# First FFN half of a two-layer backbone: weight sums formed by accumulating transfers in device memory, with modulation sums and mixer folds in their place on VectorE

## The chip, the cores and the metric

The kernel runs on one core of a Trainium2 chip. The metric is the device time of one execution in microseconds; for each kernel the median of several executions counts. TensorE (PE) does the matrix products, VectorE (DVE) and ScalarE (ACT) the elementwise work, SyncE (SP) issues transfers. GpSimd (POOL) has hardly any work in this kernel. "PEld" in the profile is TensorE's loading of weights, which overlaps its products.

## The reference

One step of a backbone of two layers over 128 context and 512 latent tokens, D = 1024. Every layer is a half-step SwiGLU FFN, a token mixer and a second half-step FFN, each between two RMS norms with shift, scale and gate from a modulation of the conditioning vectors. The mixer of the first layer is a two-dimensional Fourier transform between two projections, that of the second is attention.

```python
def _modulation(cond, w_mod, b_mod):
    m = jax.nn.silu(cond) @ w_mod + b_mod
    return m.reshape(cond.shape[0], N_MOD, D_MODEL)

def _swiglu(h, w1, w2):
    gate, up = jnp.split(h @ w1, 2, axis=-1)
    return (jax.nn.silu(gate) * up) @ w2

def _half_ffn(x, m, k, g_pre, g_post, w1, w2):
    h = _modulated_prenorm(x, g_pre, m, k)
    return x + 0.5 * m[:, 3 * k + 2, None] * _rmsnorm(_swiglu(h, w1, w2), g_post)

def _fourier_mix(h, w_in, w_out):
    b, s, _ = h.shape
    u = (h @ w_in).reshape(b, s, N_FOURIER_GROUPS, FOURIER_GROUP_DIM)
    f = jnp.fft.fft2(u.astype(jnp.float32), axes=(1, 3), norm="ortho").real
    return f.astype(h.dtype).reshape(b, s, D_MODEL) @ w_out

for i in range(DEPTH):
    m_ctx = _modulation(c_ctx[None, :], w_mod[i], b_mod[i])
    m_lat = _modulation(c, w_mod[i], b_mod[i])
...
    if i % N_MIXERS == 0:
        yp = _fourier_mix(hp, four_w_in[j], four_w_out[j])
        ys = _fourier_mix(hs, four_w_in[j], four_w_out[j])
...
```

Context and latent tokens are separate sequences in the Fourier mixer and share its weights. The FFN's inner width is 2816, that is 22 f tiles of 128.

## The kernel before, in words

**Arithmetic.** Every float32 operand is split into a high and a low part (`split`, lines 260 and 261: ACT copies the high part, DVE subtracts it), and a product is three matrix products (`mm3`, lines 274 to 276). So each weight tile passes three steps before PE can use it: SP loads a raw tile of 128 x 1024 (512 KB, line 203, "raw<-in_w" and the like in the profile), ACT writes "hi", DVE writes "lo". The raw tiles are a ring of four (NRAW), the split pairs a ring of six (NWU). `unit(i)` returns a pair and sends the ones up to three ahead through `send`, in the order of `list_units`. The results of products that are operands of later ones are split in the same way; "ring", "left", "right", "square", "total" and "rms" are names of such buffers, "main", "score", "turn" and "sum" are accumulator banks.

**First FFN half (n = 0).** Its plan is written out in `plan_ffn`. The first f tiles are done by the direct method; from f = 3 on, `w1_fast` forms the two halves of a hidden tile with seven products in place of eight, on sums of weights and sums of activations. Of the raw gate and up tiles of an f tile, four sums of 128 x 512 are needed, three for the unit "sums" (lines 228 to 230) and one for the unit "all" (line 243), all DVE's. After f = 4, 8, 12 and 16 a slice of four f tiles of w2 is run over the five token tiles, and at the end the last six.

**Background.** The modulation (the sums over `w_mod`) is cut in 128 jobs. A job loads one raw tile and runs two reductions of 1024 columns on DVE (line 478, "junk<-raw,wide"). They are taken from a list by `behind`: 36 of them between the w2 products of the first FFN half, four at its end; three in `pair_in(1)` and five in the loop over `channels`; the rest in the other sub-layers (BEHIND).

**Mixer of the first layer (n = 1).** `pair_in(0)` multiplies latent tiles 0 and 1 with the eight tiles of `four_in`, then come the context tile's odd and even products and `pair_in(1)`. Then, for each of four parts m, `positions` transforms along the tokens and `channels` along the channels, with splits of each result between the products. Then `four_out` follows: `pair_out(1)`, the context tile and `pair_out(0)`, each with its norm and its residual (`boundary`). The weights of `four_in` and `four_out` are folded when they are loaded, with two DVE operations for each (lines 237 and 238). A boundary on POOL's part takes the root of the norm (line 610), and line 633 writes the normalised tile for the next sub-layer.

**What sets the order.** The order in which instructions stand on an engine follows from the order in which the code issues them and from `high_priority` and `behind_of` around some of them; a scheduler sorts the rest by when they are expected to be ready. Each engine runs its queue in order, so that an operation which waits holds up all that stand behind it.

Of the kernel before, what the change touches and what calls it, by code (L numbers as in the profile page):

```python
# [43 lines left out]
BEHIND = (36, 0, 36, 36, 0, 8)  # L44
TURNS = (
# [107 lines left out]
class Kernel:  # L153
# [59 lines left out]
    def send(self, kind, src):  # L213
# [18 lines left out]
        elif kind.startswith("fold"):  # L232
            raw = self.raw_tile(src)
            a, b = raw[:, one], raw[:, two]
            if "rows" not in kind:
                a, b = a.rearrange("p (m c) -> p m c", m=4)[:, :, 2:], raw[:, 520:].rearrange("p (m c) -> p m c", m=4)
            nc.vector.tensor_tensor(b, a, b, op=ALU.subtract)
            nc.vector.scalar_tensor_tensor(out=a, in0=a, scalar=2.0, in1=b, op0=ALU.mult, op1=ALU.subtract)
        elif kind == "up":
            raw = self.fast["up"]  # L240
        else:
            raw, at = self.fast["gate"], two
            nc.vector.scalar_tensor_tensor(out=raw[:, two], in0=self.fast["sums"][:, two], scalar=-1.0,
                                           in1=raw[:, two], op0=ALU.mult, op1=ALU.subtract)
        n = at.stop - at.start
        if kind in ("block", "foldblock", "foldrowsblock"):
# [4 lines left out]
        return hi, lo  # L251

# [360 lines left out]
    def chain(self, n, i, pss, acc=()):  # L613
# [66 lines left out]
        with high():  # L680
# [33 lines left out]
            if n == 0:  # L714
                j, n_pieces = tiles[0], 2 * len(tiles)
                y = self.staged[:, 2 * j : 2 * j + n_pieces][:, :: -1 if j == CTX_TILE else 1]
# [4 lines left out]
                if i in (1, 2):  # L721
                    v, t, col = (2, SPECIAL, TOK + 1) if i == 1 else (5, 0, TOK)
                    for c in range(0, NCH, 2):
                        hi, lo = (h.block(part, c, 0)[:, :, col] for part in range(2))
                        self.split(hi, lo, self.staged[:, v, c : c + 2, t])
# [13 lines left out]
    def ffn(self, layer, which, base, boundary):  # L739
# [45 lines left out]
        def combine(step):  # L785
# [16 lines left out]
            if step < 2:  # L802
                t = combine.now[k] = [self.temp(("square", "total")[step]).rearrange(shape, **sizes) for _ in range(2)]
                steps = ((1, t[0], b12, b11), (2, t[1], b22, t[0]))
            else:
                t = combine.now[k]
                steps = ((3, t[0], b22, b12), (4, t[1], t[1], b21))
            for i, to, a, b in steps:
                if k == 0:
                    sums[i] = [quad(self.ring(F32R)) for _ in range(2)]  # L810
                nc.vector.tensor_tensor(to, a, b, op=ALU.subtract)
# [37 lines left out]
        def w1_fast(f, ahead):  # L849
# [28 lines left out]
            with high():  # L878
                tt(a, a, w, op=ALU.add)
# [10 lines left out]
            with high():  # L890
                nc.vector.scalar_tensor_tensor(out=q, in0=w, scalar=-1.0, in1=q, op0=ALU.mult, op1=ALU.subtract)
# [24 lines left out]
        def w2(s, tiles):  # L916
# [33 lines left out]
        for op, a, half in plan:  # L950
# [81 lines left out]
    def list_units(self):  # L1032
        io = self.io
        self.bases = []
        self.plans = {}
        for i in range(DEPTH):
            for sub in range(3):
                self.bases.append(len(self.units))
                if sub != 1:
# [3 lines left out]
                    for op, v, j in self.plans[n][1]:  # L1043
                        if op == "w2":
                            self.units.append(("plain", io["w2"][i, sub // 2, v + j]))
                        elif op in ("w1", "w1up"):
                            self.units.append(("block" if v == 3 else "plain", w1[v, int(op == "w1up")]))
                        elif op in ("sums", "again"):
                            self.units.append((op, (w1[v, 0], w1[v, 1])))
# [3 lines left out]
                if i == 0:  # L1053
                    self.units += [("foldblock" if k >= NWU else "fold", io["four_in"][k]) for k in range(NCH)]
                    self.units += [("plain", io["dft"][k]) for k in range(3)]
                    self.units += [("foldrowsblock" if u in (3, 4) else "foldrows", io["four_out"][u]) for u in range(NCH)]
# [24 lines left out]
    def fourier(self, base, boundary):  # L1081
# [44 lines left out]
        for k in range(NCH):  # L1126
            even_in(k, token(k, LAT + 64, TOK + 2), even)
# [45 lines left out]
        def positions(m):  # L1173
            ps = sums(m)
            p = [self.temp("left", F32R)[:, :322] for _ in range(2)]
            self.split(*p, ps)
            ps = diffs(m)
            q = [self.temp(kind, F32R)[:126, :384] for kind in ("square", "total")]
            self.split(*q, ps)
            return p, q  # L1180

        def channels(m, p, q):
# [6 lines left out]
            self.split(*even_at(m, 0, 322), ps)  # L1189
            ps = self.bank("score")[:, :384]  # L1190
            self.mm3(ps, mid_w[0][:126, P : 2 * P], mid_w[1][:126, P : 2 * P], *q, True, True)
            self.split(*odd_at(m, 0, 384), ps)
# [577 lines left out]
```

## Time and profile before

| | |
|---|---|
| median of three runs | 2219.53 us (2216.15 to 2219.59) |
| the profiled execution, its own time | 2218.44 us |
| its span, first to last instruction | 2216.7 us |
| mean granted TensorE clock | 0.988 |
| PE busy, DVE busy, ACT busy, POOL busy | 2173.2, 1743.1, 1179.2, 45.3 us |
| DMA traffic | 293.25 MB, mean 132 GB/s |
| first FFN half | until about 426 us |
| Fourier mixer | about 426 to 605 us |

The times come from one profiled execution. A row of the groups by line reads: line, engine, operation, output and inputs with shapes, count, then the time busy, the mean of one in ns, and the engine's idle time just before, with what ended it. A row of the table by stretches reads: the stretch and its length, the busy time (and count) on PE, PEld, DVE, ACT and POOL, the granted clock (1.00 is full), the busy share of the 16 DMA engines and their GB/s. A row of the timeline begins with the start and the duration; in square brackets stand the idle time before it and its releaser. Rows of DMA issues give the count, the size of one and the median time from issue to landing.

### The profile page before, as it was taken

The page shows a single profiled execution, that of the slowest core. Times are in us where ns is not written, and L with a number is a line of the kernel's source. Part 1 is how long each engine was busy: PE and PEld are TensorE (multiplying, and loading weights), DVE is VectorE, ACT ScalarE, POOL GpSimd, SP SyncE. Part 2 cuts the span into 40 slices and gives each one's busy share as a digit, 9 for nine tenths or more (in the row PEclk, how much of TensorE's full clock was granted, in tenths as well). Part 3 has the DMA queues.
Part 4 walks back from the last instruction along what each step waited for, and adds up shares of the span by engine and source line. Part 5 has one row for each costly group of instructions (what it writes and reads, how often), then busy time and mean ns, then how long its engine had stood idle before and what let it go on. Part 6 is the DMA issues. An engine that isn't in the chain of part 4 may idle for free.

```text
span 2216.7 us, 34573 instructions
## 1 busy us (share of the span) xinstructions
PE 2173.2 (98%) x13299; PEld 1997.3 (90%) x13299; DVE 1743.1 (79%) x3218; ACT 1179.2 (53%) x2221; POOL 45.3 (2%) x95
## 2 busy tenths in 40 slices
PE   7999999999899999999999999999999999999998
PEld 5999999977699999898998999989998899999997
DVE  5988898889798889878998898686556686766684
ACT  4544545464654545446544454466778654455452
POOL 0000000010100000001000000010000000000000
PEclk9999999998999999999999999999999999999999
DMA  8244344625324434452344444533333323322242
GB/s 315 86 143 162 134 152 139 216 86 178 116 96 138 159 132 147 148 196 99 109 147 146 141 143 146 179 99 101 111 101 110 119 81 105 115 95 77 95 129 100
DMA packets 85861, 293.25 MB, mean 132 GB/s; under 512 B 9696, under 2 KB 14656, under 8 KB 85568
## 3 DMA queue, kind: packets, MB, share of 16 engines
q1 hardware_dynamic: 85152, 290.39, 39.1%
q8 instruction: 104, 1.70, 0.3%
q10 hardware_dynamic: 544, 0.66, 0.1%
q14 instruction: 61, 0.50, 0.1%
HBM read 275.49 MB, written 11.58 MB: 130 GB/s over the span
## 4 chain that ended last, share of the span: by engine, by line
PE 89%; DVE 5%; ACT 3%; DMA 2%; issue 1%; POOL 0%; SPq 0%; DVEq 0%; POOLq 0%; ACTq 0%
PE main L275 12%; PE main L276 12%; PE main L274 12%; PE score L275 7%; PE score L276 7%; PE score L274 7%; PE turn L275 4%; PE turn L274 4%; PE sum L274 4%; PE sum L275 4%; PE turn L276 4%; PE sum L276 4%; DVE junk L478 1%; DMA raw<-in_w_mod_t 1%; PE sum L1569 1%
## 5 line engine op out<-in xcount | busy, mean ns | idle before, releaser
L260 ACT ACTIVATE hi<-raw 128x1024 fp32r<-128x1024 f32 (+1 forms) x388 | 371.1, 969 | 287.3 <-PE score L275 93.1
L261 DVE TENSOR_TENSOR lo<-raw,hi 128x1024 fp32r<-128x1024 f32 (+1 forms) x388 | 429.7, 1112 | 99.1 <-ACT hi L260 97.7
L274 PE MATMUL main<-hi,ring 128*128 128x512 f32 (+4 forms) x1089 | 412.3, 380 | 5.9 <-ACT hi L260 2.3
L275 PE MATMUL main<-lo,ring 128*128 128x512 f32 (+4 forms) x1089 | 410.8, 378 | 4.8 <-DVE lo L261 4.8
L276 PE MATMUL main<-hi,ring 128*128 128x512 f32 (+5 forms) x1089 | 410.3, 377 | 0.0
L478 DVE SCALAR_TENSOR_TENSOR junk<-raw,wide 128x1024 bf16<-128x1024 f32 x256 | 313.1, 1223 | 79.6 <-DMA raw<-in_w_mod_t 75.5
L276 PE MATMUL score<-ring,lo 128*128 128x320 f32 x916 | 283.4, 309 | 0.6 <-DVE lo L261 0.6
L275 PE MATMUL score<-ring,hi 128*128 128x320 f32 x916 | 283.7, 310 | 0.0
L274 PE MATMUL score<-ring,hi 128*128 128x320 f32 x916 | 283.3, 309 | 0.0
L274 PEld LDWEIGHTS main<-hi,ring 128*128 128x128 f32 (+2 forms) x1089 | 204.9, 189 | 47.9 <-ACT hi L260 3.6
L275 PEld LDWEIGHTS main<-lo,ring 128*128 128x128 f32 (+2 forms) x1089 | 205.9, 189 | 43.9 <-DVE lo L261 6.3
L276 PEld LDWEIGHTS main<-hi,ring 128*128 128x128 f32 (+2 forms) x1089 | 206.0, 189 | 40.5 <-issue 1.2
L274 PE MATMUL turn<-ring,hi 128*128 128x320 f32 x672 | 207.6, 309 | 3.0 <-ACT ring L260 2.9
L275 PE MATMUL turn<-ring,hi 128*128 128x320 f32 x672 | 208.3, 310 | 0.0
L274 PE MATMUL sum<-ring,hi 128*128 128x320 f32 x672 | 208.0, 310 | 0.1
L275 PE MATMUL sum<-ring,hi 128*128 128x320 f32 x672 | 207.8, 309 | 0.0
L276 PE MATMUL sum<-ring,lo 128*128 128x320 f32 x672 | 207.5, 309 | 0.0
L276 PE MATMUL turn<-ring,lo 128*128 128x320 f32 x672 | 207.0, 308 | 0.0
L942 ACT ACTIVATE y<-main 128x512 f32<-128x512 f32 x160 | 94.2, 591 | 208.2 <-PE main L276 207.0
L274 PEld LDWEIGHTS score<-ring,hi 128*128 128x128 f32 x916 | 172.4, 188 | 1.1
L276 PEld LDWEIGHTS score<-ring,lo 128*128 128x128 f32 x916 | 172.2, 188 | 1.0 <-DVE lo L261 1.0
L275 PEld LDWEIGHTS score<-ring,hi 128*128 128x128 f32 x916 | 172.3, 188 | 0.7
(318 smaller groups left out, 4138.8 us busy)
## 6 DMA issues: line engine op xcount, KB each, us to landing
raw<-in_w SPq DMA_DIRECT2D x272, 512.0 KB, 3.7
raw<-in_w_mod_t SPq DMA_DIRECT2D x128, 512.0 KB, 3.5
raw<-in_qkv SPq DMA_DIRECT2D x26, 512.0 KB, 3.5
spill<-ring SPq DMA_DIRECT2D x12, 640.0 KB, 3.3
ring<-spill SPq DMA_DIRECT2D x12, 640.0 KB, 7.4
raw<-in_bias SPq DMA_DIRECT2D x16, 448.0 KB, 3.7
first<-in_w_mod_k SPq DMA_DIRECT2D x8, 512.0 KB, 8.2
ring<-in_w_mod_k SPq DMA_DIRECT2D x8, 512.0 KB, 10.2
```

The lines of the kernel that those rows point to most:

```text
L260: a = self.nc.scalar.activation(hi, src, AF.Copy)
L261: self.last_split = a, self.nc.vector.tensor_tensor(lo, src, hi.bitcast(F32), op=ALU.subtract)
L274: mm(out, whi, xhi, start=start, stop=False)
L275: mm(out, whi, xlo, start=False, stop=False)
L276: self.latest = mm(out, wlo, xhi, start=False, stop=stop)
L478: last = self.nc.vector.scalar_tensor_tensor(out=self.junk, in0=raw, scalar=1.0, in1=self.wide[:, cond, :], op0=ALU.mult, op1=ALU.mult, ac ...
L942: nc.scalar.activation(place(i, a), ps[a], AF.Copy)
L1569: mm = nc.tensor.matmul(out, cache_v[:, ds] if k is None else v[c // 2][c % 2][:, slot, ds], probs, start=n == 0, stop=n == len(tiles) - 1)
```

## The change

For the first FFN half (`FAR = (0,)`), f tiles 5 to 21, the four weight sums are no longer DVE's. `far_sums` builds them in a tile of device memory for each f tile (four blocks of 128 x 512, the names far_78 to far_94 in the order's rows), in four stages issued from POOL: a put of four elements, taken from activations that must be there before (this holds the chain back until then), and four puts of 256 KB from the weights; two accumulating transfers from the weights; one from block to block; another one. `w1_fast(a)` issues stage 0 of f tile a + 5, stage 1 of a + 4, stage 2 of a + 3 and stage 3 of a + 2; the first tiles are begun after the third step of `combine`. SP then loads the unit "sums" from that memory as a plain tile, "up" in two pieces (one from it, one from the weights) and "all" as half a tile, 1.75 MB for an f tile in place of 1 MB. Some signs turn, so that a few operations are plain sums in place of scaled ones.

The folds of `four_in` become eight background jobs (`fold_in`): load, two DVE operations, and a write of 512 KB to device memory issued from POOL; the mixer then loads the folded tiles as they are. They are put into the list of background jobs at places 6, 12, 19, 25, 32, 38, 45 and 51. The first FFN half now takes 56 jobs (36 beside w2, one after each of 17 f tiles, three at the end): 48 modulation jobs and the eight folds. The mixer takes none. `four_out` is folded in the mixer as before.

Besides, in the mixer: the context tile's tokens are stored in reverse, with tables to match, so that one splitting of special columns goes; the odd product of `pair_in(0)` uses a bank of "score"; the splits in `positions` and `channels` are issued at high priority; `unit(at + 4)` is asked for ahead of `pair_out(1)`. PE's instructions stay the same in number and shape.

```diff
+FAR = (0,)
...
+    def fold_in(self, k):
+
+        raw = self.raw_tile(self.io["four_in"][k])
+        a, b = (t.rearrange("p (m c) -> p m c", m=4) for t in (raw[:, :512], raw[:, 520:]))
+        self.fold(a[:, :, 2:], b)
+        self.nc.gpsimd.dma_start(out=self.folded[k], in_=raw)
+
+    def far_sums(self, n, f, stage, passed):
+
+        one, two = slice(0, 512), slice(512, UNIT)
+        w1 = self.io["w1"][n // 3, n % 3 // 2, f] if (n, f) in self.far else None
+        put, add = self.nc.gpsimd.dma_start, partial(self.nc.gpsimd.dma_start, accum_op=ALU.add)
+        while w1 is not None and self.staged_sums.get((n, f), 0) <= stage:
+            t, at = self.far[n, f].rearrange("p (a k) -> p a k", a=4), self.staged_sums.get((n, f), 0)
+            if at == 0:
+                put(out=t[:1, :, :1], in_=passed[:1, 0, :4].bitcast(F32).unsqueeze(2))
+                for a, src in enumerate((w1[0][:, one], w1[0][:, one], w1[1][:, one], w1[0][:, two])):
+                    put(out=t[:, a], in_=src)
+            elif at == 1:
+                add(out=t[:, 2], in_=w1[1][:, two])
+                add(out=t[:, 0], in_=w1[1][:, one])
+            elif at == 2:
+                add(out=t[:, 1], in_=t[:, 2])
+            else:
+                add(out=t[:, 3], in_=t[:, 1])
+            self.staged_sums[n, f] = at + 1
...
-            nc.vector.scalar_tensor_tensor(out=raw[:, two], in0=self.fast["sums"][:, two], scalar=-1.0,
-                                           in1=raw[:, two], op0=ALU.mult, op1=ALU.subtract)
+            nc.vector.tensor_tensor(raw[:, two], self.fast["sums"][:, two], raw[:, two], op=ALU.add)
...
-                if n == 0 and s == len(SLICES) - 1 and tiles[0] == 0 and f < f0 + 4:
+                if n == 0 and s == len(SLICES) - 1 and tiles[0] == 0 and f < f0 + 3:
...
             elif op == "combine":
                 combine(a)
+                if a == 3:
+                    for stage in range(4):
+                        for f in range(7 if stage < 3 else 6):
+                            self.far_sums(n, f, stage, sums[4][0])
...
             elif op == "fast":
                 w1_fast(a, half)
+                for i in range(4):
+                    self.far_sums(n, a + 5 - i, i, g[a])
+                if n == 0 and a > 4:
+                    self.behind()
...
+                        elif n in FAR and op in ("sums", "up", "all") and (n, v, "again") not in self.plans:
+                            if op == "sums":
+                                self.far[n, v] = self.dram.tile([P, 2 * UNIT], F32, tag=f"far{n}_{v}", name=self.name("far"))
+                            t = self.far[n, v]
+                            self.units.append({"sums": ("plain", t[:, :UNIT]), "all": ("half", t[:, UNIT + 512 :]),
+                                               "up": ("pieces", (t[:, UNIT : UNIT + 512], w1[v, 1][:, 512:]))}[op])
...
-                    self.units += [("foldblock" if k >= NWU else "fold", io["four_in"][k]) for k in range(NCH)]
+                    self.folded = [self.dram.tile([P, UNIT], F32, tag=f"fold{k}", name=self.name("fold")) for k in range(NCH)]
+                    self.units += [("block" if k >= NWU else "plain", self.folded[k]) for k in range(NCH)]
...
-            es, o = [self.bank() for _ in range(2)], self.bank()
+            es, o = [self.bank() for _ in range(2)], self.bank("main" if p else "score")
             for k in range(NCH):
-                if p and k % 3 == 1:
-                    self.behind()
...
-            self.split(*p, ps)
+            with high():
+                self.split(*p, ps)
...
-            self.behind((2, 2, 1, 0)[m])
...
+        self.unit(at + 4)
         pair_out(1)
...
+        for k in range(NCH):
+            self.background.insert(6 + 13 * k // 2, partial(self.fold_in, k))
```

More of the change, by code (lines that the diff above doesn't have):

```diff
@@ L233, in send @@
             raw = self.raw_tile(src)
[L234 to L238, printed above, removed]
+            self.fold(raw[:, one], raw[:, two])
+        elif kind == "pieces":
+            raw = self.raw.tile([P, UNIT], F32, tag="raw", name=self.name("raw"))
+            for a, piece in zip((one, two), src):
+                nc.sync.dma_start(out=raw[:, a], in_=piece)
+        elif kind == "half":
+            raw, at = self.raw_tile(src, 512), one
         elif kind == "up":
@@ L720, in chain @@
                     self.ready = self.split(split(hi), split(lo), y[:, :, c : c + 2].rearrange("p v c t -> p c v t"))
-                if i in (1, 2):
-                    v, t, col = (2, SPECIAL, TOK + 1) if i == 1 else (5, 0, TOK)
+                if i == 1:
                     for c in range(0, NCH, 2):
-                        hi, lo = (h.block(part, c, 0)[:, :, col] for part in range(2))
-                        self.split(hi, lo, self.staged[:, v, c : c + 2, t])
+                        hi, lo = (h.block(part, c, 0)[:, :, TOK] for part in range(2))
+                        self.split(hi, lo, self.staged[:, 2, c : c + 2, SPECIAL])
                 tiles = ()
@@ L878, in w1_fast @@
             with high():
-                tt(a, a, w, op=ALU.add)
+                tt(a, a, w, op=ALU.subtract)
             if f in opened:
@@ L1034, in list_units @@
         self.bases = []
-        self.plans = {}
+        self.plans, self.far, self.staged_sums = {}, {}, {}
         for i in range(DEPTH):
@@ L1126, in fourier @@
         for k in range(NCH):
-            even_in(k, token(k, LAT + 64, TOK + 2), even)
+            even_in(k, token(k, LAT + 63, TOK + 1), even)
         plain, ends = self.ring(F32)[:64, :504], self.ring(F32R)
@@ L1175, in positions @@
             p = [self.temp("left", F32R)[:, :322] for _ in range(2)]
-            self.split(*p, ps)
+            with high():
+                self.split(*p, ps)
             ps = diffs(m)
             q = [self.temp(kind, F32R)[:126, :384] for kind in ("square", "total")]
-            self.split(*q, ps)
+            with high():
+                self.split(*q, ps)
             return p, q
@@ L1188, in channels @@
                 mm(x5, mid_w[0][:, 256 + 72 * m : 328 + 72 * m], p[i], start=m == i == 0, stop=False)
-            self.split(*even_at(m, 0, 322), ps)
+            with high():
+                self.split(*even_at(m, 0, 322), ps)
             ps = self.bank("score")[:, :384]
             self.mm3(ps, mid_w[0][:126, P : 2 * P], mid_w[1][:126, P : 2 * P], *q, True, True)
-            self.split(*odd_at(m, 0, 384), ps)
+            with high():
+                self.split(*odd_at(m, 0, 384), ps)
         ready = positions(0)
@@ L1707, in host_inputs @@
     ctx = np.arange(64)
+    back = ctx[::-1]
     big = np.zeros((3, P, UNIT))
@@ L1726, in host_inputs @@
     small = np.zeros((P, 208))
-    small[:64, :64] = -wave(np.sin, ctx, ctx, CTX) / 128
+    small[:64, :64] = -wave(np.sin, back, ctx, CTX) / 128
     small[:64, 64:128] = -small[:64, :64]
```

27 lines of the change are left out of this document (18 added, 9 removed).

## The prediction

> **What bounds the kernel now.** I began with the page's busy shares and the granted clock.
>
> ```profile
> span 2216.7 us, 34573 instructions
> PE 2173.2 (98%) x13299; PEld 1997.3 (90%) x13299; DVE 1743.1 (79%) x3218; ACT 1179.2 (53%) x2221; POOL 45.3 (2%) x95
> PEclk9999999998999999999999999999999999999999
> ```
>
> PE is busy for 98% of the span, so what it idles is 2216.7 − 2173.2 = 43.5 us. The rest of what can be won is work done at a lowered clock: the one slice with an 8 is the tenth, 499 to 554 us, which is the mixer. Next I cut the part that the change touches into stretches (first FFN half from slice 0 of w2 on, then the mixer).
>
> ```profile
> core 0: us, PE busy (x) PEld busy (x) DVE busy (x) ACT busy (x) POOL busy (x), PEclk, DMA share, GB/s
> 104.00:426.00 322.00, 322.00 (x1916) 300.21 (x1915) 284.59 (x469) 156.47 (x245) 0.00 (x0) 1.00 0.44 147
> 440.00:472.00 32.00, 31.10 (x149) 24.96 (x148) 28.04 (x58) 24.26 (x62) 5.66 (x8) 1.00 0.11 34
> 472.00:490.00 18.00, 13.39 (x59) 9.85 (x58) 17.42 (x32) 9.20 (x21) 1.13 (x2) 0.81 0.36 118
> 490.00:520.00 30.00, 30.00 (x207) 26.58 (x205) 26.10 (x40) 16.81 (x31) 0.00 (x0) 1.00 0.49 166
> 520.00:555.00 35.00, 31.37 (x117) 23.84 (x116) 32.62 (x58) 11.46 (x20) 0.00 (x0) 0.71 0.58 191
> 555.00:566.00 11.00, 8.12 (x29) 5.30 (x28) 5.80 (x11) 4.32 (x10) 0.00 (x0) 0.84 0.38 135
> 566.00:605.00 39.00, 35.26 (x160) 26.74 (x159) 31.39 (x66) 30.41 (x67) 5.10 (x9) 0.91 0.26 90
> ```
>
> In the FFN (first row) PE is busy 322 of 322 us at clock 1.00, although DVE is busy for 284.59, or 88%. Removing DVE work there is worth nothing by itself. In the mixer PE waits and is throttled. Its weight loads name the waits; the last figures in brackets are the idle time and its releaser.
>
> ```profile
> 473.91 0.19 PEld L274 LDWEIGHTS main<-hi,ring 128*128 128x128 f32 x1 [1.45 <-DVE ring L633]
> 483.05 0.29 PEld L275 LDWEIGHTS main<-lo,ring 128*128 128x128 f32 x1 [3.85 <-DVE lo L261]
> 522.10 0.19 PEld L274 LDWEIGHTS main<-hi,ring 128*126 128x126 f32 x1 [2.06 <-DVE rms L261]
> 539.49 0.19 PEld L274 LDWEIGHTS score<-left,hi 128*128 128x128 f32 x1 [2.29 <-DVE ring L261]
> 560.00 0.30 PEld L274 LDWEIGHTS main<-hi,ring 128*128 128x128 f32 x2 [2.78 <-ACT hi L260]
> ```
>
> All but the last are DVE, which is full there: 17.42 of 18 us and 32.62 of 35 us. Part of what fills it has nothing to do with the chain:
>
> ```profile
> L478 DVE SCALAR_TENSOR_TENSOR junk<-raw,wide 128x1024 bf16<-128x1024 f32 x17 | 20.7, 1216 | 0.3 <-DMA raw<-in_w_mod_t 0.2
> L237 DVE TENSOR_TENSOR raw<-raw 128x512 f32<-128x512 f32 (+1 forms) x15 | 10.1, 683 | 0.0
> L238 DVE SCALAR_TENSOR_TENSOR raw<-raw 128x512 f32<-128x512 f32 (+1 forms) x15 | 10.1, 683 | 0.1
> ```
>
> These are DVE's groups between 440 and 566 us: modulation sums (L478) and mixer folds (L237, L238), 40.9 us together.
>
> **The change part by part.** First the FFN.
>
> ```profile
> L478 DVE SCALAR_TENSOR_TENSOR junk<-raw,wide 128x1024 bf16<-128x1024 f32 x75 | 91.8, 1223 | 22.6 <-DMA raw<-in_w_mod_t 21.2
> L243 DVE SCALAR_TENSOR_TENSOR raw<-sums,raw 128x512 f32<-128x512 f32 x17 | 11.7, 688 | 0.2
> L228 DVE TENSOR_TENSOR sums<-raw,raw 128x512 f32<-128x512 f32 x16 | 11.0, 688 | 0.1
> ```
>
> It removes four weight sums for each of 17 f tiles (L228, L229, L230, L243): 68 × 0.69 = 47 us of DVE. It adds eight modulation jobs, 16 × 1.22 = 19.5 us, and eight folds of two operations, 16 × 0.68 = 10.9 us. DVE's net in the FFN is −16.6 us, and since PE there is at 322 of 322 us the term is 0. What hides it is PE's own work; if the sums came late, that cover would go (rivals). In the mixer, DVE loses eight jobs (16 × 1.22 = 19.5 us) and eight `four_in` folds (10.9 us); the eight `four_out` folds stay. This is where the time must come from.
>
> *472 to 490 us* (the first pair of latent tiles). At stake are the idle time, 18 − 13.39 = 4.6 us, and 0.19 × 13.39 = 2.5 us of throttling: 7.1 us. The wait of 3.85 us is for the low half of a mixer weight. In PE's order before, that point reads as follows; main_4548 to main_4550 are the three accumulators of `pair_in(0)`, hi_4555 and lo_4556 the two halves of its fourth weight, main_4689 the context tile's odd product.
>
> ```order
> L274 MATMUL main_4550<-hi_4555,ring_4415 128x504
> L276 MATMUL main_4689<-hi_4212,ring_4412 64x504
> L274 MATMUL main_4689<-hi_4232,ring_4415 64x504
> L275 MATMUL main_4689<-lo_4233,ring_4415 64x504
> L276 MATMUL main_4689<-hi_4232,ring_4416 64x504
> L274 MATMUL main_4689<-hi_4555,ring_4415 64x504
> L275 MATMUL main_4548<-lo_4556,ring_4415 128x256
> ```
>
> And after, with hi_4793 and lo_4794 for that weight, main_4919 and main_4982 for the context's odd and even products:
>
> ```order
> L308 MATMUL score_4790<-hi_4793,ring_4663 128x504
> L309 MATMUL main_4919<-lo_4481,ring_4663 64x504
> L310 MATMUL main_4919<-hi_4480,ring_4664 64x504
> L308 MATMUL main_4919<-hi_4793,ring_4663 64x504
> L310 MATMUL main_4982<-hi_4462,ring_4660 66x256
> L308 MATMUL main_4982<-hi_4480,ring_4663 66x256
> L309 MATMUL main_4982<-lo_4481,ring_4663 66x256
> L310 MATMUL main_4982<-hi_4480,ring_4664 66x256
> L308 MATMUL main_4982<-hi_4793,ring_4663 66x256
> L309 MATMUL main_4788<-lo_4794,ring_4663 128x256
> ```
>
> The even context product has moved ahead of the waiting instruction, and one accumulator has moved to the score bank. Of the folds this stretch held four, so as many of L238:
>
> ```profile
> 472.00:490.00 18.00, 2.64 (x4) 0.81 0.36 118
> ```
>
> That is 5.3 of DVE's 17.42 us (the second column is L237's busy time), more than the wait of 3.85. But the weight's low half still stands in DVE's queue behind the context tile's boundary, so not all goes. I take 5 (bounds 2, the 1.45 us wait and little more, and 7.1).
>
> *520 to 555 us* (`positions` and `channels`). At stake: idle 35 − 31.37 = 3.6 and throttled 0.29 × 31.37 = 9.1, so 12.7 us. The clock is halved by short waits in sequence:
>
> ```profile
> 540.00:545.00 5.00, 5.00 (x14) 2.94 (x13) 5.00 (x10) 0.93 (x2) 0.00 (x0) 0.54 0.59 186
> 545.00:550.00 5.00, 5.00 (x14) 3.76 (x13) 4.55 (x11) 1.38 (x2) 0.00 (x0) 0.50 0.76 239
> ```
>
> After the wait of 2.29 us PE runs at about half clock without a pause for ten microseconds. DVE's queue before, in this place (left and total are the inputs of the DFT products, raw_50xx the folds, junk the modulation sums):
>
> ```order
> L261 TENSOR_TENSOR left_4992<-main_4981,left_4991 128x322
> L261 TENSOR_TENSOR total_5004<-main_4995,square_5003 126x384
> L478 SCALAR_TENSOR_TENSOR junk,mod<-raw_5007,wide 128x1024
> L237 TENSOR_TENSOR raw_5015<-raw_5015 128x512
> L478 SCALAR_TENSOR_TENSOR junk,mod<-raw_5007,wide 128x1024
> L238 SCALAR_TENSOR_TENSOR raw_5015<-raw_5015 128x512
> L478 SCALAR_TENSOR_TENSOR junk,mod<-raw_5011,wide 128x1024
> L261 TENSOR_TENSOR left_5050<-main_5039,left_5049 128x322
> ```
>
> and after:
>
> ```order
> L295 TENSOR_TENSOR left_5210<-main_5199,left_5209 128x322
> L295 TENSOR_TENSOR rms_5152<-main_5153,rms_5151 8x322
> L295 TENSOR_TENSOR total_5222<-main_5213,square_5221 126x384
> L257 TENSOR_TENSOR raw_5225<-raw_5225 128x512
> L257 TENSOR_TENSOR raw_5275<-raw_5275 128x512
> L258 SCALAR_TENSOR_TENSOR raw_5225<-raw_5225 128x512
> L258 SCALAR_TENSOR_TENSOR raw_5275<-raw_5275 128x512
> L295 TENSOR_TENSOR left_5260<-main_5249,left_5259 128x322
> ```
>
> Between one split of `left` and the next the modulation sums are gone (3 × 1.22 us), two folds more have come (2 × 0.68): DVE's lead is shorter by some 2.3 us, the size of the wait. What L478 took of the whole stretch:
>
> ```profile
> 520.00:555.00 35.00, 12.21 (x20) 0.71 0.58 191
> ```
>
> DVE keeps 32.62 − 12.21 = 20.4 us, against 31.37 × 0.71 = 22.3 us of PE work at full clock. The two are nearly level, so I take 9.5 of 12.7 (bounds 4, the two waits of 2.06 and 2.29 us without the clock, and 12.7).
>
> [...]
>
> *555 to 566 us*: idle 2.9, throttled 0.16 × 8.12 = 1.3, so 4.2 us. The wait of 2.78 us is for ACT's half of a weight whose transfer is now asked for ahead of `pair_out(1)`. I take 3 (0 to 4.2). *566 to 605 us* and *440 to 472 us*: nothing in the change reaches the waits on ACT there; 0.
>
> Sum: 5 + 9.5 + 3 = 17.5 us against the profiled execution's own 2218.44 us, so 2200.9; the median of the three runs (2219.53) is 1.1 us above that execution, so 2202. Bounds of the three terms together are 6 and 24 us; the first with everything low, the second with every wait gone; I use 10 to 24 for this case, 2195 to 2209.
>
> **What must hide: the transfers.** For each f tile the added work is one small put, four puts of 256 KB, and four accumulating adds of 256 KB, all issued from POOL, which issues no transfer before.
>
> ```order
> L275 DMA far_83<-ring_1310 4x1x1 [waits DMASW6_49,Activation_49]
> L277 DMA far_83<-in_w 128x512 [waits DMASW6_49]
> L277 DMA far_83<-in_w 128x512
> L277 DMA far_83<-in_w 128x512 [waits DMASW1_49]
> L277 DMA far_83<-in_w 128x512
> L280 DMA far_83<-in_w 128x512 [waits DMASW7_49,DMASW3_49]
> L279 DMA far_83<-in_w 128x512 [waits DMASW4_49,DMASW1_49]
> L282 DMA far_83<-far_83 128x512 [waits DMASW5_49,DMASW4_49,DMASW0_49]
> L284 DMA far_83<-far_83 128x512 [waits DMASW5_49,DMASW2_49]
> L275 DMA far_84<-ring_1454 4x1x1 [waits Activation_49]
> ```
>
> This is POOL's queue for f tile 10 (far_83) and the start of tile 11 (far_84). The stages of one tile stand in sequence and wait for each other, and tile 11 waits behind them: the staging five tiles ahead does not overlap tiles here. The chain is thus five landings long.
>
> ```profile
> gate<-rms SPq DMA_DIRECT2D x2, 8.0 KB, 2.6
> total<-gate SPq DMA_DIRECT2D x2, 256.0 KB, 3.6
> raw<-in_w SPq DMA_DIRECT2D x50, 512.0 KB, 3.9
> 148.19 0.49 DVE L261 TENSOR_TENSOR ring<-right,ring 128x320 fp32r<-128x320 f32 x1
> 399.38 0.69 DVE L228 TENSOR_TENSOR sums<-raw,raw 128x512 f32<-128x512 f32 x1
> ```
>
> Small put 2.6, four puts about 3.9 + 1 (twice the bytes of the 3.9 row, at the rate between the rows), two adds 3.6, one add 3.6, then the last, which nobody on POOL waits for: 14.7 us, and I take 15 to 18 with POOL's issuing, which no row prices. Tiles 10 to 21 (12 chains) may begin when tile 5's activations are split (148.7 us), and the last sums are wanted at 399.4: 250.7 / 12 = 20.9 us each. So it holds, with 3 to 6 us each to spare.
>
> **The rivals.** *A: the clock stays low.* The splits still wait, or PE's work there is too thin to win its clock back; only the low bounds of the terms come: 2 + 4 + 0 = 6 us, 2218.44 − 6 + 1.1 = 2213.5. For it: 20.4 against 22.3 us of DVE and PE. Against it: 490 to 520 us ran at 1.00 with DVE at 26.10 of 30. Chance 0.14.
>
> *B: the DMA engines fill.* In the FFN they moved 147 GB/s. Added between 104 and 426 us: 17 × 0.75 MB of larger loads, 4 MB of modulation rows, 8 MB for folds, 17 × 8 × 0.25 = 34 MB for puts and adds: some 59 MB on 47, or 330 GB/s. The first 60 us show where it ends:
>
> ```profile
> GB/s 0 155 377 305 392 401 415 426 418 412 412 407 412 407 412 412 410 423 404 410 415 376 373 435 410 401 404 418 268 33 0 5 0 19 325 229 126 104 246 0
> raw<-in_w SPq DMA_DIRECT2D x11, 512.0 KB, 9.7
> ```
>
> About 410 GB/s, with 9.7 us to landing. Four raw tiles must carry five loads per f tile, and a run takes 12.4 us a tile:
>
> ```profile
> 237.63 0.49 DVE L871 TENSOR_TENSOR left<-score,left 128x320 f32<-128x320 f32 x1
> 250.02 0.48 DVE L871 TENSOR_TENSOR left<-score,left 128x320 f32<-128x320 f32 x1
> L261 DVE TENSOR_TENSOR lo<-raw,hi 128x1024 fp32r<-128x1024 f32 (+1 forms) x67 | 72.5, 1085 | 5.3 <-ACT hi L260 5.0
> L260 ACT ACTIVATE hi<-raw 128x1024 fp32r<-128x1024 f32 (+1 forms) x388 | 371.1, 969 | 287.3 <-PE score L275 93.1
> ```
>
> That is 9.9 us a load, less 3 us (1.09 + 0.97 for the two halves, 1 for queueing): a landing slower than 6.9 us stalls PE. At 7.9 us each of 17 tiles loses 5/4 us, 21 us, and the gain is gone: about 2222. [...] Chance 0.11.
>
> *C, on the other side: the chain of sums is late.* If an accumulating add takes longer than a load, or the landings double as in the first 60 us (a chain of five near 10 us would be 40), c passes 20.9 us. At 24 us the last sums are 12 × 3.1 = 37 us late. SP waits on the device-memory tile with the w2 and modulation loads queued behind it, and PE stops: 2202 + 37 = 2239. It decides from c = 20.9, and costs more than the gain from 22.4. For it: no row shows an accumulating transfer or POOL's issuing. Against it: at 0.44 of the engines the landings are 2.6 to 3.9 us. Chance 0.17.
>
> *D: nothing moves*, since the waits return behind others: 2219. Chance 0.03.
>
> **How the numbers follow.** The forecast has 0.55, A 0.14, B 0.11, C 0.17, D 0.03. A measurement of this kernel tells changes from 0.2%, 4.4 us, on. Faster: 0.55 + 0.14 + 0.01 of B = 0.70; same: 0.06 of B, 0.03 of C, all of D = 0.12; slower: 0.14 of C, 0.04 of B = 0.18. The predicted time is 2202. The range runs from 2193 (every wait gone, 24 us, and 2 of the 4.6 us that PE idles in the two stretches set at 0) to 2222, which takes in A, B and D, and leaves C.
>
> **What would show it.** Right: in the stretches of the mixer no idle time over 1 us on DVE, clock 0.9 or more from `positions` to `pair_out(1)`, no L478 there; PE without a wait in the FFN with DMA share 0.8 to 0.9; landings of weights below 6.9 us; far chains of 15 to 18 us. Wrong: PE idle in the FFN behind `raw<-far` (C) or behind weights whose landings are above 7 us (B), or a clock of 0.7 in the mixer with DVE free (A).

## The result, and the profile after

| | before | after |
|---|---|---|
| median | 2218.28 us | 2370.89 us (2366.24 to 2374.66) |
| ratio | | 1.0688, 95% interval 1.0666 to 1.071 |
| span of the profiled execution | 2216.7 us | 2370.1 us |
| first norm's root in the mixer (POOL) | 443.9 us | 615.8 us |
| from there to the mixer's last root | 161.6 us | 142.0 us |

The change makes the kernel 6.9% slower. The two last rows divide it: the first FFN half has become 172 us longer, the mixer some 20 us shorter. The page of the changed kernel:

```profile
span 2370.1 us, 34971 instructions
PE 2184.2 (92%) x13299; PEld 2007.9 (85%) x13299; DVE 1704.2 (72%) x3146; ACT 1178.3 (50%) x2217; POOL 151.0 (6%) x256
PEclk9989697979999999999999999999999999999999
DMA  7687778777443344434434434442333323223332
```

PE idles 2370.1 − 2184.2 = 186 us in place of 43.5, and both the low digits of the clock and the 7s and 8s of DMA stand in the first ten slices. The stretches, with the FFN from the same start to its new end, and the parts of the mixer that roughly answer to the rows at 472, 490 and 520 us before:

```profile
104.00:576.00 472.00, 327.23 (x1805) 299.67 (x1805) 263.79 (x436) 151.28 (x238) 95.48 (x144) 0.84 0.78 215
650.00:662.00 12.00, 8.82 (x46) 7.56 (x45) 9.93 (x12) 3.57 (x6) 0.09 (x1) 0.86 0.59 189
662.00:692.00 30.00, 30.00 (x200) 25.82 (x199) 22.27 (x33) 17.90 (x33) 0.00 (x0) 1.00 0.43 147
692.00:720.00 28.00, 28.00 (x139) 21.47 (x138) 23.18 (x38) 14.62 (x30) 0.54 (x1) 1.00 0.42 139
```

In the mixer, `positions` and `channels` now run at clock 1.00 without a pause (last row), where they had 0.71. In the FFN, PE is busy for 327 of 472 us. What PE and SP wait for between 60 and 620 us (total, times, longest):

```profile
PE sum L310 <- DVE lo L295: 82.0, 4, 28.9
PE score L308 <- ACT left L902: 50.4, 4, 19.7
PE turn L308 <- DVE left L910: 13.6, 9, 4.7
```

```profile
SPq L204 <- DVE lo L295: 147.3, 61, 25.1
SPq L239 <- DMA fold<-raw: 90.4, 3, 32.5
SPq L204 <- DMA fold<-raw: 51.3, 5, 19.4
SPq L204 <- DMA far<-far: 7.0, 1, 7.0
```

The first row is SP's wait for a raw tile that has yet to be split; before the change it was 156.0 us between 104 and 426 us, so it tells nothing of the loss. New are 141.7 us for writes of folded tiles, and only 7 us for a chain of sums. One such wait can be followed from engine to engine. DVE ends a fold at 216.3; POOL is in a chain:

```profile
215.66 0.68 DVE L258 SCALAR_TENSOR_TENSOR raw<-raw 128x504 f32<-128x504 f32 x1
```

```profile
219.40 0.85 POOL L280 DMA_DIRECT2D far<-in_w  x1 [1.66 <-DMA far<-in_w]
228.47 0.82 POOL L282 DMA_DIRECT2D far<-far  x1 [4.28 <-issue]
239.49 0.83 POOL L265 DMA_DIRECT2D fold<-raw  x1
```

The write leaves 23 us after the fold. Until it has landed, 6.5 us later, the folded tile keeps one of the four raw tiles. SP, whose next load needs that tile, issues nothing from 217.90 to 246.04:

```profile
217.90 0.33 SPq L204 DMA_DIRECT2D raw<-far  x1
246.04 0.33 SPq L239 DMA_DIRECT2D raw<-far  x1
246.94 1.33 SPq L204 DMA_DIRECT2D raw<-in_w_mod_t  x3
```

Behind it stand the loads of the modulation jobs, for which DVE waits, and behind these sums stands, in DVE's queue, the low half that PE needs:

```profile
251.86 1.23 DVE L512 SCALAR_TENSOR_TENSOR junk<-raw,wide 128x1024 bf16<-128x1024 f32 x1 [24.43 <-DMA raw<-in_w_mod_t]
278.16 1.22 DVE L295 TENSOR_TENSOR lo<-raw,hi 128x1024 fp32r<-128x1024 f32 x1
```

```profile
279.43 0.64 PE L310 MATMUL sum<-ring,lo 128*128 128x320 f32 x1 [23.46 <-DVE lo L295]
```

The chain is longer than forecast too. Starts of chains (the small puts) in a run of f tiles, on POOL:

```profile
303.58 0.55 POOL L275 DMA_DIRECT2D far<-ring  x1 [23.35 <-ACT ring L294]
331.04 0.83 POOL L275 DMA_DIRECT2D far<-ring  x1
349.87 0.82 POOL L275 DMA_DIRECT2D far<-ring  x1
370.54 0.84 POOL L275 DMA_DIRECT2D far<-ring  x1
425.46 0.55 POOL L275 DMA_DIRECT2D far<-ring  x1 [21.65 <-ACT ring L294]
```

Four tiles take 121.9 us, of which POOL waits 21.65 for PE's activations: 25 us for a chain. The landings, in the stretch 104 to 426 us:

```profile
far<-in_w POOLq DMA_DIRECT2D x66, 256.0 KB, 6.4
raw<-in_w_mod_t SPq DMA_DIRECT2D x32, 512.0 KB, 6.6
far<-far POOLq DMA_DIRECT2D x24, 256.0 KB, 5.8
far<-ring POOLq DMA_DIRECT2D x12, 0.0 KB, 5.8
```

Even the put of a few bytes lands after 5.8 us, where I had taken 2.6.

### The profile page after: what moved, and what is told of

The parts are those of the page before. It is cut to its first block, busy times and chain, and to the rows that moved or that the text cites. A ratio compares the mean times of both kernels' runs of the same rounds, so it can differ in the third digit from the quotient of the medians.

```text
span 2370.1 us, 34971 instructions
## 1 busy us (share of the span) xinstructions
PE 2184.2 (92%) x13299; PEld 2007.9 (85%) x13299; DVE 1704.2 (72%) x3146; ACT 1178.3 (50%) x2217; POOL 151.0 (6%) x256
## 4 chain that ended last, share of the span: by engine, by line
PE 69%; DVE 3%; ACT 3%; DMA 1%; issue 1%; POOL 0%; DVEq 0%; POOLq 0%; ACTq 0%
PE main L308 10%; PE main L309 10%; PE main L310 10%; PE score L310 5%; PE score L309 5%; PE score L308 5%; PE turn L309 3%; PE sum L309 3%; PE turn L308 3%; PE sum L310 3%; PE sum L308 3%; PE turn L310 3%; PE sum L1625 1%; PE score L1558 1%; DMA raw<-in_w_mod_t 1%
## 5 line engine op out<-in xcount | busy, mean ns | idle before, releaser
L294 ACT ACTIVATE hi<-raw 128x1024 fp32r<-128x1024 f32 (+1 forms) x405 | 390.5, 974 | 500.8 <-PE score L309 117.3
L295 DVE TENSOR_TENSOR lo<-raw,hi 128x1024 fp32r<-128x1024 f32 (+1 forms) x405 | 451.3, 1118 | 176.4 <-ACT hi L294 175.1
L309 PE MATMUL main<-lo,ring 128*128 128x512 f32 (+4 forms) x1083 | 405.5, 375 | 4.2 <-DVE lo L295 4.1
L308 PE MATMUL main<-hi,ring 128*128 128x512 f32 (+4 forms) x1083 | 408.9, 378 | 0.0
L310 PE MATMUL main<-hi,ring 128*128 128x512 f32 (+4 forms) x1083 | 404.1, 374 | 0.0
L309 PEld LDWEIGHTS main<-lo,ring 128*128 128x128 f32 (+1 forms) x1083 | 203.1, 188 | 42.6 <-DVE lo L295 4.9
L308 PEld LDWEIGHTS main<-hi,ring 128*128 128x128 f32 (+2 forms) x1083 | 203.0, 187 | 40.2 <-issue 0.5
L310 PEld LDWEIGHTS main<-hi,ring 128*128 128x128 f32 (+1 forms) x1083 | 202.8, 187 | 39.9 <-issue 0.2
L308 PE MATMUL turn<-ring,hi 128*128 128x320 f32 x672 | 210.8, 314 | 16.5 <-DVE left L910 13.6
L308 PEld LDWEIGHTS score<-ring,hi 128*128 128x128 f32 x916 | 174.3, 190 | 53.1 <-ACT left L902 52.0
L309 PE MATMUL turn<-ring,hi 128*128 128x320 f32 x672 | 210.4, 313 | 0.0
L310 PEld LDWEIGHTS sum<-ring,lo 128*128 128x128 f32 x672 | 128.7, 192 | 83.1 <-DVE lo L295 83.1
```

The source lines that it names most:

```text
L294: a = self.nc.scalar.activation(hi, src, AF.Copy)
L295: self.last_split = a, self.nc.vector.tensor_tensor(lo, src, hi.bitcast(F32), op=ALU.subtract)
L308: mm(out, whi, xhi, start=start, stop=False)
L309: mm(out, whi, xlo, start=False, stop=False)
L310: self.latest = mm(out, wlo, xhi, start=False, stop=stop)
```

## Experiments

Theory 1: the raw tile that the folded tile's write holds. Theory 2: the chain's length. Theory 3: the time that the added bytes take on the DMA engines. The first four runs move the folds or their writes, and take the sums away, singly and together.

**The folds back in the mixer, the sums still in device memory** (2312.94 us, 1.0435, 1.0416 to 1.0454)

```diff
-        for k in range(NCH):
-            self.background.insert(6 + 13 * k // 2, partial(self.fold_in, k))
-                    self.units += [("block" if k >= NWU else "plain", self.folded[k]) for k in range(NCH)]
+                    self.units += [("foldinblock" if k >= NWU else "foldin", io["four_in"][k]) for k in range(NCH)]
-                if n == 0 and a > 4:
+                if n == 0 and a > 12:
                     self.behind()
```

> The folds of four_in go back to the mixer, nothing else is written from POOL than the chains of sums; the 48 modulation jobs stay in the first FFN half. Theory 1 (a folded tile keeps one of the four raw tiles until POOL, behind a chain of sums, has issued its write; SP waited 141.7 us on such writes): the FFN is again as before, the mixer loses some of its gain of 19 us to 10.9 us of folds, 2203 to 2215 us. Theory 2 (the chain of sums is too long by itself, 25 us for an f tile against the 20.9 that there is room for): 12 x 4.1 = 49 us remain, 2250 to 2265. Theory 3 (the DMA engines are full, share 0.8): 8 of 59 MB less, over 2330.

No theory alone gives 2313. 58 us went with the folds, and 95 us stay. SP's waits now name the chain:

```profile
SPq L204 <- DVE lo L299: 135.2, 55, 25.1
SPq L204 <- DMA far<-far: 127.2, 15, 18.9
```

**The folded tile written by SP** (2308.01 us, 1.0414, 1.0398 to 1.0429)

```diff
-        self.nc.gpsimd.dma_start(out=self.folded[k], in_=raw)
+        self.nc.sync.dma_start(out=self.folded[k], in_=raw)
```

> The changed kernel with one line different: the folded tile is written by SP in place of POOL, so that it no longer stands behind a chain; the bytes are the same. Theory 1: the raw tile comes free some 6 us after the fold, 2198 to 2208 us. Theory 2: 2240 to 2255. Theory 3: no change, 2360 to 2375.

One changed word takes 63 us away, with the same bytes. SP's waits for the folded tiles' writes fall from 141.7 to 28.4 us. So theory 1 is right for 63 of the 153 us, and it is the queue that cost, not the folding. With the folds in the mixer (the run above) nothing is held either: POOL no longer waits for PE, and a chain takes 28 us, against 20.9 of room. Eleven chains of that run lie between these rows.

```profile
165.87 0.78 POOL L279 DMA_DIRECT2D far<-ring  x1
473.67 0.81 POOL L279 DMA_DIRECT2D far<-ring  x1
```

**No sums in device memory** (2224.31 us, 1.0042, 1.0025 to 1.0059), and **that with the folds in the mixer** (2216.61 us, 0.9999, 0.999 to 1.0009)

```diff
-FAR = (0,)
+FAR = ()
```

> FAR is empty: the weight sums are DVE's again, while folds and modulation jobs stay where the change put them (POOL's queue holds nothing but the eight writes of folded tiles). Theory 1: the writes leave at once; DVE in the FFN has 284.6 + 30.4 = 315 of 322 us, which just fits: 2198 to 2212. A rival, that DVE at 98% delays the sums and with them PE: 2215 to 2240. Theories 2 and 3 say the same as 1 here, since the chains and 34 MB are gone.

> FAR is empty and the folds are back in the mixer; of the moves only the eight modulation jobs and the rearranged mixer remain. DVE in the FFN has 284.6 + 19.5 = 304 of 322 us: PE stays without a wait there; the mixer has the folds (10.9 us) again: 2203 to 2215 us. If most of the gain in the mixer comes from the missing folds, 2212 or more.

With POOL's chains gone the kernel is within 0.4% of the time before the change, and no faster. From the first root on, the second takes 143.9 us, but this root comes 17 to 23 us later than before (460.7 in the second). It is not the same point of PE's work in these runs: 2631 and 2634 products stand ahead of it, 2607 before. At the 2607th product they are about 17 and 9 us late, and from there to the mixer's last root they take about 13 and 10 us less than before. I take DVE's load for the cause of the delay; where it acts is seen in a later run (jobs beside the w2 slices).

Six runs then part the remaining loss, all made from the kernel of the first run (2312.94).

**Stages in turn**: POOL's queue kept in the order of the calls, oldest tile first (2270.37 us, 1.0226, 1.0205 to 1.0246)

```diff
+        def put(**kw):
+            with self.behind_of(*([self.far_last] if self.far_last else [])):
+                self.far_last = self.nc.gpsimd.dma_start(**kw)
+        add = partial(put, accum_op=ALU.add)
...
-                for i in range(4):
+                for i in range(3, -1, -1):
                     self.far_sums(n, a + 5 - i, i, g[a])
```

> The kernel with the folds in the mixer, with POOL's queue kept in the order in which the stages are called, oldest tile first: the last stages of two tiles, then the first adds of a third, then the puts of a fourth. The same transfers and bytes; two landings for an f tile in sequence in place of five. Theory 2: an f tile takes POOL 14 to 18 us, less than the 20.9 there is room for, 2205 to 2225 us. Theory 3: the engines need 1.1 of the FFN's 322 us, so 2245 to 2290.

43 us less: that much was the sequence of the chain (theory 2). 71 us stay above the kernel without chains (below), and SP still waits 36.8 us for sums. DMA is at 0.93 of its engines:

```profile
104.00:426.00 322.00, 289.45 (x1573) 263.63 (x1572) 216.93 (x356) 128.98 (x200) 89.76 (x135) 0.93 0.93 257
```

**Sums formed but not read** (2248.41 us, 1.0129, 1.0101 to 1.0156), and **no chains at all** (2199.08 us, 0.9913, 0.9895 to 0.9932)

```diff
-                            self.units.append({"sums": ("plain", t[:, :UNIT]), "all": ("half", t[:, UNIT + 512 :]),
-                                               "up": ("pieces", (t[:, UNIT : UNIT + 512], w1[v, 1][:, 512:]))}[op])
+                            t = w1[v, 0]
+                            self.units.append({"sums": ("plain", t), "all": ("half", t[:, 512:]),
+                                               "up": ("pieces", (t[:, :512], w1[v, 1][:, 512:]))}[op])
...
-        w1 = self.io["w1"][n // 3, n % 3 // 2, f] if (n, f) in self.far else None
+        w1 = self.io["w1"][n // 3, n % 3 // 2, f] if (n, f) in self.far and f < 18 else None
```

> Made from the kernel with the folds in the mixer (2312.9 us). POOL forms the sums of f tiles 5 to 17 in device memory as there, but SP loads the same shapes from the unsummed weights, so that nothing waits for a chain; the sums that the products need are left out. Theory 2 (the products wait for a chain of 28 us for an f tile): no stall of PE is left, 2195 to 2212 us. Theory 3 (the transfers fill the DMA engines; from its records a byte that POOL moves takes 1.65 times the engine time of one that SP loads, and the FFN would need 1.1 of them): the loads still land late, 2250 to 2300.

> As the kernel before it, without any of POOL's transfers: SP's larger loads alone, and VectorE without the sums, which are left out. Both theories: PE without a wait in the first FFN half, 2195 to 2210 us; this is what the change could have brought had the sums been free.

The second has `f < 0` in that last line. It shows what the forecast rested on: sums for nothing, PE busy all through the FFN, the first root at 444.1, a mixer of 143.0 us, 2199.

```profile
104.00:426.00 322.00, 321.86 (x1914) 299.73 (x1913) 266.07 (x438) 157.95 (x245) 0.00 (x0) 1.00 0.60 200
```

The first forms the sums of f tiles 5 to 17 alone, 13 chains in place of 17. It says that 49 us are lost although no product waits for a chain. Its loads land later:

```profile
raw<-in_w SPq DMA_DIRECT2D x43, 512.0 KB, 5.5
raw<-in_w_mod_t SPq DMA_DIRECT2D x42, 512.0 KB, 6.1
```

against, without chains:

```profile
raw<-in_w SPq DMA_DIRECT2D x50, 512.0 KB, 3.5
raw<-in_w_mod_t SPq DMA_DIRECT2D x47, 512.0 KB, 4.3
```

**Plain transfers in place of the accumulating ones**, read by the products as before (2245.78 us, 1.0115, 1.01 to 1.013), and the same **where nothing reads them** (2224.43 us, 1.0031, 1.002 to 1.0041)

```diff
-        put, add = self.nc.gpsimd.dma_start, partial(self.nc.gpsimd.dma_start, accum_op=ALU.add)
+        put, add = self.nc.gpsimd.dma_start, self.nc.gpsimd.dma_start
```

> The kernel with the folds in the mixer, each of the four accumulating transfers replaced by a plain one of the same blocks in the same order, so that no sum is formed: this prices the accumulation. If a transfer that adds costs no more than one that copies, 2305 to 2320 us, unchanged. If reading the destination costs a third of its time, c falls by 4 us and the time by 12 x 4 to 2265. Theory 2 and 3 differ here only by what the accumulation takes from the engines.

> The same kernel (2248.4 us) with full blocks, its accumulating transfers replaced by plain ones; nothing waits for them, and the sums that the products need are left out. If accumulation takes engine time beyond a copy's: 2215 to 2232, between the two. If it only lengthens a chain for those who wait: 2245 to 2252.

Accumulation is dear: 67 us of the 2313, and 24 of the 49 us where nothing waits for it. So it takes engine time, beyond the landing that a chain waits for.

**An eighth of the bytes**, nothing read (2203.32 us, 0.9935, 0.992 to 0.995)

```diff
-                    put(out=t[:, a], in_=src)
+                    put(out=t[:, a, :64], in_=src[:, :64])
...
-                add(out=t[:, 1], in_=t[:, 2])
+                add(out=t[:, 1, :64], in_=t[:, 2, :64])
```

> The kernel whose sums are formed but not read (2248.4 us), with every block that POOL moves cut to 64 of its 512 columns: the same number of transfers, waits and issues, an eighth of the bytes; the sums that the products need are left out. If the loss of 49 us against no chains (2199.1) is the time that bytes take on the DMA engines: 2199 to 2210. If it comes of the number of transfers or of POOL's issuing: 2235 to 2250.

With the same number of transfers the loss falls from 49 to 4 us. It is the bytes' time on the engines (theory 3), not POOL's issuing.

The last runs ask whether some version beats both kernels.

**Where the mixer's gain comes from**: the rearranged mixer alone, all jobs and folds where they were (2221.81 us, 1.0019, 1.001 to 1.0028)

```diff
+                if p and k % 3 == 1:
+                    self.behind()
...
+            self.behind((2, 2, 1, 0)[m])
```

> No sums in device memory, folds and modulation jobs where they were before the change: only the rearranged mixer is left (context tile reversed, score bank for the odd product, high priority for the splits, earlier request of a weight). If the gain of the mixer comes from the eight jobs that left it: 2213 to 2220. If from the order: 2200 to 2208.

The mixer takes 164 us, 2.5 more than before the change. The reversed context tile, the score bank, the priorities and the earlier request bring nothing by themselves. In the rearranged mixer with its folds, it was the eight modulation jobs' leaving that took it to 143 (no chains). Whether their leaving does as much without the rearrangement, no run shows.

**Jobs spread beside the w2 slices** (2222.51 us, 1.002, 1.0011 to 1.0029), and **folds there too** (2234.41 us, 1.0076, 1.0062 to 1.0089); both with the sums on DVE

```diff
-BEHIND = (36, 0, 36, 36, 0, 8)
+BEHIND = (44, 0, 36, 36, 0, 8)
...
-                if n == 0 and a > 12:
-                    self.behind()
```

> Made from the kernel without sums in device memory and with the folds in the mixer (2216.6 us; its mixer took 143.9 us against 161.6 before, but its first FFN half 16.8 us more). The eight modulation jobs that it runs after f tiles 13 to 21 are spread beside the w2 slices (44 there, four at the end as before). If the FFN lost to a queue of jobs at its end, that is gone: 2199 to 2207 us. If it lost to VectorE's total (304 of 322 us), nothing changes: 2212 to 2220.

> As the kernel before it, with the eight folds of four_in among the jobs beside w2 too, written to device memory from POOL, which has no chains (52 jobs beside w2, four at the end). VectorE has 315 of 322 us in the FFN. If the place of the jobs was what cost: 2197 to 2206. If VectorE's total decides: 2215 to 2228.

The place of the jobs is not what costs. PE idles 14.6 us of the same 322 in the first:

```profile
104.00:426.00 322.00, 307.42 (x1758) 282.63 (x1758) 281.79 (x468) 143.03 (x228) 0.00 (x0) 0.98 0.43 144
```

Its DVE has a share of 0.88 over the stretch, as before the change: a mean that hides the places where DVE is full. PE's waits come in pairs at 148 and 151, 230 and 235, 314 and 318, 398 and 402 us, each in the f tiles that follow a w2 slice. There DVE works off what has gathered:

```profile
304.00:314.00 10.00, 8.26 (x55) 7.74 (x54) 9.97 (x22) 2.65 (x5) 0.00 (x0) 1.00 0.40 130
```

Before the change such a stretch (294 to 304 us) had DVE at 9.90 of 10 us and PE still at 10. So eight jobs more find no room there; that the same holds in the two runs above that keep the sums on DVE is argued from this one.

**Sums in device memory for every other tile** (2237.03 us, 1.0095, 1.0073 to 1.0118) and **for one in four** (2223.08 us, 1.0026, 1.0015 to 1.0038)

```diff
-                        elif n in FAR and op in ("sums", "up", "all") and (n, v, "again") not in self.plans:
+                        elif n in FAR and op in ("sums", "up", "all") and (n, v, "again") not in self.plans and v % 2:
```

> The kernel with the folds in the mixer (2312.9 us), with sums in device memory for the nine odd f tiles only; VectorE forms the others. Theory 3: the engines need 0.60 + 9/17 of 0.52, about 0.87 of the FFN, under their limit, so that little is lost: 2200 to 2215. Theory 2: a chain of 28 us has 38 us: the same. If every transfer from POOL delays the loads in proportion, half of e1's loss stays: 2255.

> As the kernel with sums in device memory for every other f tile (2237.0 us), for tiles 5, 9, 13, 17 and 21 alone, four of which follow a w2 slice: VectorE has 304 - 13.8 = 290 of 322 us, the engines 0.48 + 5/17 of 0.52, about 0.63. If the two have a common optimum: 2200 to 2212. If VectorE's total still costs: 2213 to 2220. If any transfer of POOL delays the loads in proportion: 2220 or more.

Neither is faster than before. The first loses 38 us against the kernel without chains at a DMA share of 0.74, well short of full. Which part of that is landings and which is DVE's half of the sums, no run tells apart.

**The sums as POOL's own additions** on SBUF tiles (2252.53 us, 1.0148, 1.0123 to 1.0174), and **with the folds early** (2262.22 us, 1.0197, 1.018 to 1.0214)

```diff
+            who = nc.gpsimd if self.sent < self.bases[1] else nc.vector
-            nc.vector.tensor_tensor(raw[:, one], gate[:, one], up[:, one], op=ALU.add)
+            who.tensor_tensor(raw[:, one], gate[:, one], up[:, one], op=ALU.add)
```

> No sums in device memory, folds in the mixer (2216.6 us): the four sums of an f tile in the first FFN half are POOL's own additions on SBUF tiles, in place of VectorE's. VectorE is relieved by 47 us without a byte more for the DMA engines. If VectorE's total is what costs the FFN 17 us in the kernel before: 2197 to 2206. If POOL's additions are slow (over 3 us each) or slow VectorE down: 2215 to 2260.

> The same with the folds of four_in in the first FFN half as the change has them, written by SP: the change without its transfers for sums. The mixer gains some 2 us more than with the folds; VectorE has 279 of 322 us in the FFN: 2195 to 2204. If POOL's additions are slow: 2215 to 2260.

An addition takes POOL 1.3 to 1.5 us, less than I had feared, and the result is slower all the same. Two things are seen. DVE waits for the sums: an f tile's three additions stand in sequence and take more than twice as long as on DVE (1454 to 1524 ns against some 690), and DVE idles 32.5 us ahead of their low halves (1.3 before the change). And some of DVE's own operations beside them take longer: the split of a hidden tile 1205 ns here. How much each costs, no run tells apart.

```profile
L230 POOL TENSOR_TENSOR sums<-raw,raw 128x512 f32<-128x512 f32 x15 | 22.9, 1524 | 234.5 <-DMA raw<-in_w 149.4 <-DVE lo L301 72.8 <-DVE left L916 12.4
L301 DVE TENSOR_TENSOR lo<-sums,hi 128x1024 fp32r<-128x1024 f32 x15 | 19.1, 1274 | 32.5 <-ACT hi L300 32.5
L301 DVE TENSOR_TENSOR ring<-right,ring 128x320 fp32r<-128x320 f32 x14 | 16.9, 1205 | 0.0
```

The split took 486 before the change:

```profile
L261 DVE TENSOR_TENSOR ring<-right,ring 128x320 fp32r<-128x320 f32 x17 | 8.3, 486 | 0.0
```

None of the kernels that form the sums beats the kernel before.

## Why the prediction was wrong

**The mixer's sum held, its terms less well.** 17.5 us were forecast; the mixer became 19.6 us shorter, and the kernel without chains ran in 2199.1 us against the 2202 of the forecast, with the folds still in the mixer. The next rows hold 405 products before (first two) and as many after (last two): from the start of `pair_in(0)` to the transposes behind it, and from there to the first product that follows `channels`.

```profile
471.07:495.16 24.09, 19.48 (x95) 14.80 (x94) 21.41 (x37) 12.11 (x28) 1.13 (x2) 0.86 0.43 138
495.16:563.56 68.40, 61.89 (x310) 50.26 (x308) 59.83 (x99) 29.16 (x54) 0.00 (x0) 0.83 0.51 174
643.57:666.22 22.65, 19.30 (x105) 15.52 (x104) 17.59 (x28) 11.26 (x24) 1.13 (x2) 0.92 0.49 163
666.22:716.17 49.95, 49.95 (x300) 42.05 (x298) 40.80 (x61) 28.72 (x53) 0.00 (x0) 1.00 0.43 140
```

The first pair, forecast at 5 us, brought 1.4, or some 3 if ten products that have moved into it are taken out (10 × 0.18 us). Its wait of 3.85 us stayed (3.44 now, for the same low half), as its place in DVE's queue had suggested. The two later terms, forecast at 12.5 together, brought 18.5, or some 17. So it is in part luck that the sum came out near. One cause was put wrong, the order of PE: the rearrangement alone gave nothing. The clock gave about 12 of the 19.6 us, an estimate from the busy time and the granted clock (0.88 over 145.9 busy us of the mixer before, 0.96 over 134.0 after).

**The step that failed first: what POOL's queue holds up.** The prediction counted the folded tiles' 4 MB of writes, and not that each write, behind a chain on POOL, keeps a raw tile. Its list of what waits behind a chain ended with the w2 and modulation loads. The write lost 63 us, and appears in no rival.

**The second: the chain's price (rival C).** The side and the point of decision, 20.9 us, were right; the price was not. I took the landings from rows of a DMA system at a share of 0.44 (2.6 to 3.9 us), and so 15 to 18 us, while the same change brought it to 0.8 and more. With the folds in the mixer (share 0.87) the four landings that a chain waits for took 5.7 to 7.4 us each: 28 us with POOL's issuing. B and C were treated as separate cases, though the load of B sets the price of C. By 12 × (28 − 20.9) = 85 us, C would have been 2287; the run with the folds in the mixer, where it acts without the folds' writes, took 2313, so C's own price does not cover the loss.

**The third: bytes as the measure of the engines (rival B).** The sum of 330 GB/s against 410 left room. But bytes are not alike. These rows give packets, MB and the share of the engines' time between 104 and 426 us: POOL's queue with adds and without (the two kernels in which nothing reads the sums), then SP's without chains.

```profile
q0 software_dynamic: 10542, 23.67, 36.8%
q0 software_dynamic: 7372, 23.09, 23.8%
q1 hardware_dynamic: 21462, 64.03, 59.5%
```

That is 200, 301 and 334 GB/s. If half of the first were copies, an adding byte goes at about 149 GB/s, half a copy's rate. By this estimate the adds of 17 tiles (17.8 MB) take 120 us, the copies 59, and SP's 64 MB 192: 371 of 322 us, and still 349 if two of the chains fall ahead of the stretch. That is more than there is. That POOL's bytes and SP's add up on the engines was assumed in the forecast, and no row of before could show it. The runs do: when chains run that nothing reads, POOL's queue (36.8%) and SP's (51.2%) together make the share of 0.88, and landings of SP's loads of `in_w` rise from 3.5 to 5.5 us.

**Rivals A and D** did not occur. What the forecast did not name is that DVE's room in the FFN could not be used in these runs: at PE 322 of 322 and DVE 284.6 I had taken moved jobs as free because the sums paid for them. They do, but only as long as the sums cost nothing elsewhere; with the sums on DVE and the folds in the mixer, the eight jobs cost about 9 us there and bring about 10 in the mixer.

## What to carry to other kernels

A queue that runs in order holds more than its own work (here a write that left 23 us after its fold, and 63 us of the time): for each instruction moved to it, ask what buffer it keeps until it is issued, and who needs that buffer. A latency is to be taken at the load that the change itself makes (SP's loads of `in_w` landed here after 3.5 us at a DMA share of 0.60 and after 5.5 us at 0.88), and the load in engine time, not in bytes (POOL's queue moved 200 GB/s here with adds, 301 without). A mean share of 88% on an engine does not show room beside another engine that never pauses; look for the stretches where it is full.

## What the runs showed of the hardware

An accumulating transfer between blocks of device memory took about twice the engine time of a copy (149 against 301 GB/s, an estimate from the shares above). A put of 16 bytes from SBUF, issued by POOL, landed after 5.8 us at a DMA share of 0.8. POOL's additions of 128 x 512 on SBUF tiles took 1.3 to 1.5 us each, and one kind of DVE's operations beside them took 2.5 times as long in the mean (1205 against 486 ns); beside POOL's transfers the same kind took 482.
